# Two products issued later in the gating heads, and six landing places instead of three for the output weights of layer A

## The chip, the cores and the metric

The kernel runs on one core of a Trainium2 chip. The metric is the device time of one execution, in microseconds. Before the change it is 2045.86 us, the median of three runs (2043.93 to 2048.65). The core has an engine for matrix products (TensorE, PE in the profile; its weight loads are PEld), a vector engine (VectorE, DVE), a scalar engine (ScalarE, ACT), a general engine (GpSimd, POOL) and a queue that here only starts DMAs (SyncE, SP). Each engine runs its own instructions strictly in program order and waits for the others by semaphores.

## The reference, cut to what matters

Two layers, each `x <- x + norm(mixer(norm(x)))`, on x of 1024 x 1024 floats. Layer A is a gated unit, layer B dilated attention. Only layer A and its end matter here:

```
z = h @ w_in;  u, v, g = split(z)            # 2048 columns each
v = layer_norm(gelu(v), vn_g, vn_b)          # over 2048 columns
sg = w_s[h] @ v[chunk, head h] + b_s[h]      # 16 heads, 8 chunks of 128 rows
y = gelu(u) * sg * silu(g);  out = y @ w_out # 2048 -> 1024
x = x + rms_norm(out) * ...;  h for layer B = rms_norm(x)
```

## The kernel before, in words

**Precision.** Each fp32 operand is split into a high part and the rest, and each product is three matmuls (high x high, high x rest, rest x high). The splits cost ACT one copy and DVE one subtraction for each 128 x 512 tile.

**The order.** It is written by a small planner (class `Plan`): every matmul that is emitted moves a clock of its own forward, and actions put into a heap with `plan.at` or `plan.after` are emitted, on whatever engine they belong to, when that clock passes their time. These times only set the order of instructions; the engines run as fast as their waits let them.

**Pieces.** Weights (and, at the end of layer A, the rows of y) come as pieces of 128 x 512 through class `Pieces`. A piece from DRAM is loaded by SP into a landing place, a tile `raw` of which there are three; ACT and DVE split it into a tile `wt` (eight of them, so splitting runs up to eight pieces ahead of TensorE); when the split is emitted its place counts as free and the next load is emitted. The load waits on its queue until the split has really happened. `source(raw, nr, lo_pool, slack)` tells the object where places come from, how many there are, which pieces GpSimd splits, and how long a place is kept back after its split.

**Heads of layer A (`head`, line 792; `spatial`, line 673).** For each of 16 heads, u and g come from seven products in Strassen's manner (forms a11, a12, s2, s1, s3, a22, s4; 12 matmuls of 512 columns each), of which partial sums x in a PSUM bank psD are copied out by ACT (`snap`) before the next form adds to them. Beside the next head's products the planner puts the spatial part of the head: `ws_tr` transposes w_s[h] (tile wsr), ACT and DVE split it into `wst`; `ws_sum` multiplies it by a matrix of ones, to get row sums, and DVE makes t (from psT, the factors vgb and the bias bsr); `v_load`, `v_norm`, `v_split` bring v (tiles vr, vs); `mix` multiplies vs by wst (psS), and DVE makes sg and the product ya, which `y_out` stores. `ws_load`, on ACT's queue, fetches w_s and b_s of the head after the next. `vgb_tr` (line 631) transposes the norm factors vn_g and vn_b once, before the first use of vgb. The form tiles of the heads, and the pieces of summed weights, lie in a pool `fm`.

**End of layer A (line 932 on).** Four blocks (two halves of the rows, two halves of the columns), each of 16 steps; a step takes a piece of y and a piece of w_out and issues 12 matmuls into four banks. At the end of a block ACT copies each bank out (yo) and squares it. The banks of the blocks are DDOO, SSTT, DDOO, DDSS. After blocks two and four, `post` emits for each of four row tiles the norm, the residual, the second norm and the transposes of h for layer B (psT from xr), on DVE, ACT and TensorE. Then layer B's values are computed (`v_bank`) from 16 pieces of four loads each, in banks psD again.

Of the kernel before, what the change touches and what calls it, by code (L numbers as in the profile page):

```python
# [12 lines left out]
F32 = mybir.dt.float32  # L13
# [8 lines left out]
P = 128  # L22
# [196 lines left out]
def encoder_block(ctx: ExitStack, tc: tile.TileContext, x, norm_pre, norm_post, a_w_in, a_w_s,  # L219
# [8 lines left out]
    plan = Plan()  # L228
# [12 lines left out]
    pc = Pieces(nc, plan, lambda: wpool.tile([P, 2, 512], F32R, name="wt"), 8)  # L241

    def bank(tag):
        return ps.tile([P, 512], F32, name="ps" + tag, tag=tag)
# [7 lines left out]
    def bcast_row(ap, off, n):  # L252
        return bass.AP(tensor=ap.tensor, offset=ap.offset + off, ap=[[0, P], [1, n]])
# [23 lines left out]
    def bmm(o, l, r, start, stop):  # L277
        mm(o, l, r, start, stop)

    def tr(o, i):  # L280
        nc.tensor.transpose(o, i, ident)  # L281
        plan.now += 0.109

    def act(o, i, f=AF.Copy, **k):
        nc.scalar.activation(o, i, f, **k)  # L285

    def tt(o, a, b, op, e=None):
        (e or nc.vector).tensor_tensor(o, a, b, op=op)  # L288

    def stt(o, a, s, b, op0, op1):  # L290
        nc.vector.scalar_tensor_tensor(o, a, s, b, op0=op0, op1=op1)  # L291
# [66 lines left out]
    def new_h():  # L358
        return (hpool.tile([P, 8, S], F32R, name="hTh", tag="hTh"),
                hpool.tile([P, 8, S], F32R, name="hTl", tag="hTl"))  # L360
# [114 lines left out]
    for i in range(8):  # L475
        b = bank("D")
        for k in range(8):
# [5 lines left out]
            while n > 0 and norms:  # L483
                weight, f = norms.pop(0)
# [36 lines left out]
    fms = ExitStack()  # L521
# [111 lines left out]
        nc.tensor.transpose(b[:, :2 * NH], vrow, ident[:2 * NH, :2 * NH])  # L633
        act(vgb.rearrange("p a h -> p (a h)"), b[:, :2 * NH])

    plan.after(2.0, vgb_tr)

    def dense_cols(o, w, s0, n):

# [31 lines left out]
    def spatial(h, ug, t0):  # L671
        vs, T = {}, ws.pop(h)

        def ws_tr():
            b = bank("T")
            tr(b[:, :128], T["w"])
            T["wt"] = sp.tile([P, 2, P], F32R, name="wst")
            act(T["wt"][:, 0], b[:, :128])
            tt(T["wt"][:, 1], b[:, :128], T["wt"][:, 0].bitcast(F32), OP.subtract)

        def ws_sum():
            b = bank("T")
            bmm(b[:, :256], ones, T["wt"].rearrange("p a q -> p (a q)"), True, True)
            T["t2"] = sp.tile([P, P], F32, name="t2")
            stt(T["t2"], b[:, :128], vgb[:, 1, h:h + 1], T["b"], OP.mult, OP.add)
            stt(T["t2"], b[:, 128:256], vgb[:, 1, h:h + 1], T["t2"], OP.mult, OP.add)

        def v_load():
            vs["r"] = sp.tile([P, 8, P], F32, name="vr", bufs=1)
            nc.sync.dma_start(vs["r"], va[h])  # L690

        def v_norm(i):
            act(vs["r"][:, i], vs["r"][:, i], AF.Identity, scale=lnr[:, i:i + 1], bias=lnb[:, i:i + 1])

        def v_split(e):
            if e == 0:
                vs["v"] = sp.tile([P, 2, 8, P], F32R, name="vs", bufs=1)
                act(vs["v"][:, 0], vs["r"])
            else:
                tt(vs["v"][:, 1], vs["r"], vs["v"][:, 0].bitcast(F32), OP.subtract)  # L700

        def mix(cc):
            b = bank("S")
            for k in range(2):
                c = 2 * cc + k
                bmm(b[:, 256 * k:256 * k + 256], vs["v"][:, 0, c], T["wt"].rearrange("p a q -> p (a q)"),
                    True, False)
                bmm(b[:, 256 * k:256 * k + 256], vs["v"][:, 1, c], T["wt"].rearrange("p a q -> p (a q)"),
                    False, True)
            g = sp.tile([P, 2, P], F32, name="sg")  # L710
            b4 = b.rearrange("p (c a q) -> p c a q", c=2, a=2)
            t2 = T["t2"][:, None, :].to_broadcast([P, 2, P])
            stt(g, b4[:, :, 0], vgb[:, 0, h:h + 1], t2, OP.mult, OP.add)
            stt(g, b4[:, :, 1], vgb[:, 0, h:h + 1], g, OP.mult, OP.add)

            if cc == 0:
                vs["y"] = sp.tile([P, S], F32, name="ya", bufs=1)
            y = vs["y"].rearrange("p (t c b) -> p c t b", t=8, c=8)[:, 2 * cc:2 * cc + 2]
            tt(y, g.rearrange("p c (b t) -> p c t b", t=8),
               ug[:, 256 * cc:256 * cc + 256].rearrange("p (c b t) -> p c t b", c=2, t=8), OP.mult)  # L720
            if cc == 3:
                plan.after(2.0, y_out)

        def y_out():
            nc.sync.dma_start(ya[h], vs["y"])
            done_a.add(h)
            pc.pump()

        plan.at(t0, v_load)
        plan.at(t0 + 0.2, ws_tr)  # L730
        for i in range(8):
            plan.at(t0 + 3.5 + 0.35 * i, v_norm, i)
        plan.at(t0 + 6.5, v_split, 0)
        plan.at(t0 + 7.6, v_split, 1)
        plan.at(t0 + 2.5, ws_sum)
        plan.at(t0 + 4.0, ws_load, h + 2)
        return mix

    def y_a(kt, sh):
# [23 lines left out]
    lo_pool = set()  # L763
# [42 lines left out]
    def head(h, mixes):  # L806
        if h + 1 < NH:
            plan.after(0.8, w_load, h + 1)
        u = sp.tile([P, S], F32, name="us")
        c0, c1 = slice(0, 512), slice(512, 1024)  # L810
        x, z, y = bank("D"), bank("O"), None
        g = {}

        def snap(nm):
            g[nm] = sp.tile([P, 512], F32, name=nm, bufs=1)
            act(g[nm], x)

        def gate(c, o, nm):

            g[c] = g[nm]  # L820
            tt(g[c], o, g[nm], OP.add)

        def gated(c, i):
            tt(u[:, c], u[:, c], g[i], OP.mult)

        form_mm(x, "a11", True)
        snap("p1")
        form_mm(z, "a12", True)
        tt(u[:, c0], z, g["p1"], OP.add)
        form_mm(x, "s2")  # L830
        snap("u2")
        y = bank("O")
        form_mm(y, "s1", True)
        form_mm(x, "s3")
        snap("u3")
        gate(1, y, "u3")
        for f in mixes[:2]:
            f()
        form_mm(x, "a22")
        act(u[:, c1], x, AF.Gelu_apprx_tanh)  # L840
        act(u[:, c0], u[:, c0], AF.Gelu_apprx_tanh)
        for f in mixes[2:3]:
            f()
        form_mm(y, "s4")
        gate(0, y, "u2")
        for f in mixes[3:]:
            f()
        for dt, c in ((0.0, 1), (0.9, 0)):
            plan.after(dt, act, g[c], g[c], AF.Silu)
        plan.after(1.4, gated, c1, 1)  # L850
        plan.after(2.4, gated, c0, 0)
        mix = spatial(h, u, plan.now + 0.5)
        return [lambda cc=cc: mix(cc) for cc in range(4)]

    mixes = []
    for h in range(NH):
        mixes = head(h, mixes)
    plan.after(10.0, lambda: [f() for f in mixes])


    def out_mm(b, y, w, t, first, last):
# [57 lines left out]
    def open_chain():  # L919
        plan.until(lambda: len(done_a) == NH)  # L920
        sps.close()
        fms.close()
        cp["pool"] = chs.enter_context(tc.tile_pool(name="cp", bufs=2, side="right", reuse_waits="tile"))
        cp["gp"] = cp["pool"].tile([P, D], F32, name="gp", bufs=1)
        nc.sync.dma_start(cp["gp"], bcast_row(norm_post, 0, D))
        cp["gq"] = cp["pool"].tile([P, D], F32, name="gq", bufs=1)
        nc.sync.dma_start(cp["gq"], bcast_row(norm_pre, D, D))
        cp["n"] = 0
        hnew["h"], hnew["l"] = new_h()
        pc.source(raw, 3)  # L930

    plan.after(25.0, open_chain)
    for sh, ch, tags in ((0, 0, "DDOO"), (0, 1, "SSTT"), (1, 0, "DDOO"), (1, 1, "DDSS")):
        bs = [bank(t) for t in tags]
# [13 lines left out]
                post(4 * sh + t, POST_EVERY[sh][0] + POST_EVERY[sh][1] * t)  # L948


    pc.source(raw, 3, lo_pool, 2.0)
    hTh, hTl = hnew["h"], hnew["l"]

    def v_alloc():
# [479 lines left out]
    def open_b2():  # L1434
        chs.close()
        st = ExitStack()
        B2["s"] = st
        B2["p"] = st.enter_context(tc.tile_pool(name="b2", bufs=2, side="right", reuse_waits="tile"))


    for t in range(0, 8, 2):
        for c in range(4):
            vch.setdefault(c, [])
            v_bank(c, t, t == 6, None if c else lambda i: plan.until(lambda: cp["n"] > i))
    plan.drain()
    open_b2()
    xws.close()
    b1s = ExitStack()
    b1 = b1s.enter_context(tc.tile_pool(name="b1", bufs=2, reuse_waits="tile"))

# [175 lines left out]
```

## Time and profile before

| what | value |
|---|---|
| median of three runs | 2045.86 us |
| the profiled execution, its span | 2045.38 us, 2043.6 us |
| TensorE, its weight loads | 96%, 81% of the span |
| DVE, ACT, GpSimd | 65%, 54%, 16% |
| heads of layer A | about 203 to 578 us |
| end of layer A, four blocks | 578.1 to 797 us |

TensorE is busy nearly throughout; what it loses is in short waits, and in stretches in which its granted clock is at the lower of its two levels, 1.2 GHz instead of 2.4 GHz (a granted clock of 0.83 over 20 us means that it was at the half for 6.8 us of them, so that 3.4 us are lost beside the waits).

### The profile page before, as it was taken

Reading aid. Unit: us, or ns where it says so; the run is one execution under the profiler, and the core shown is the slowest. Engines: PE = TensorE matmul, PEld = TensorE weight load, DVE = VectorE, ACT = ScalarE, POOL = GpSimd, SP = SyncE. Lnnn points to the kernel's source line nnn. Section 1 sums busy time; section 2 is a strip of 40 time slices with the busy share of each in tenths; the row PEclk is TensorE's granted clock in tenths of the full one; section 3 lists DMA queues with packets and bytes.
Section 4 is the critical chain, followed back from the end, with each engine's and each line's share of the span. In section 5 each row is a group of like instructions: output and inputs, shape, how many; then the busy total and the mean of one; then the engine's idle time right before and its main releaser. Section 6 shows DMA issues by size and latency. Waiting matters only on the chain.

```text
span 2043.6 us, 30630 instructions
## 1 busy us (share of the span) xinstructions
PE 1962.9 (96%) x10617; PEld 1665.1 (81%) x10617; DVE 1325.6 (65%) x3051; ACT 1108.5 (54%) x2455; POOL 332.9 (16%) x394
## 2 busy tenths in 40 slices
PE   8999899999989988999999999999999999999998
PEld 5887777777767667999898888898888888787876
DVE  6455577787764576526567576585675766868747
ACT  5223466666654455225656665656566556576722
POOL 0001322232100000011003021130120310413121
PEclk9999999999989999999999999999999999999999
DMA  4334444433245556331223142241331422313277
GB/s 174 105 114 125 126 142 127 133 122 99 87 134 181 185 191 203 107 115 50 76 77 106 52 112 66 70 129 47 101 102 52 114 64 86 113 47 104 79 222 273
DMA packets 246024, 235.57 MB, mean 115 GB/s; under 512 B 18843, under 2 KB 203835, under 8 KB 245868
## 3 DMA queue, kind: packets, MB, share of 16 engines
q1 hardware_dynamic: 235068, 219.97, 35.4%
q10 hardware_dynamic: 10800, 13.63, 1.9%
q8 instruction: 84, 1.38, 0.3%
q14 instruction: 72, 0.59, 0.1%
HBM read 188.03 MB, written 57.04 MB: 120 GB/s over the span
## 4 chain that ended last, share of the span: by engine, by line
PE 68%; DVE 14%; DMA 9%; ACT 4%; issue 3%; SPq 0%; POOL 0%; ACTq 0%; DVEq 0%
PE psD L270 50%; PE psO L270 8%; PE psS L270 5%; DVE wt L178 4%; PE psT L281 3%; DMA raw<-in_a_w_out_dram 3%; DVE sg L291 3%; PE psT L270 2%; ACT wt L176 1%; DMA raw<-ya 1%; DVE ya L288 1%; DMA toep<-vec 1%; DVE o L288 1%; DMA raw<-in_b_w_in_dram 1%; DMA vr<-va 1%
## 5 line engine op out<-in xcount | busy, mean ns | idle before, releaser
L270 PE MATMUL psD<-hTh,wt 128*128 128x512 f32 x2176 | 722.3, 396 | 3.7 <-ACT u L285 3.6
L270 PEld LDWEIGHTS psD<-hTh,wt 128*128 128x128 f32 x2176 | 401.1, 189 | 72.2 <-ACT u L285 4.5
L270 PE MATMUL psD<-hTl,wt 128*128 128x512 f32 x1088 | 433.3, 398 | 0.0
L270 PE MATMUL psD<-wt,hTh 128*128 128x256 f32 (+1 forms) x1760 | 360.6, 301 | 9.6 <-ACT psD L285 4.9
L178 DVE TENSOR_TENSOR wt<-raw,wt 128x512 fp32r<-128x512 f32 x316 | 215.2, 702 | 190.2 <-ACT wt L176 188.3
L270 PEld LDWEIGHTS psD<-wt,hTh 128*128 128x128 f32 x1760 | 285.2, 193 | 21.7 <-ACT psD L285 5.3
L176 ACT ACTIVATE wt<-raw 128x512 fp32r<-128x512 f32 x328 | 197.7, 627 | 189.0 <-DMA raw<-in_a_w_out_dram 53.0
L285 ACT ACTIVATE xs<-xs,st 128x256 f32<-128x256 f32 (+2 forms) x384 | 176.7, 461 | 174.9 <-DVE st L1155 173.8
L270 PE MATMUL psD<-wt,hTl 128*128 128x256 f32 (+1 forms) x880 | 265.7, 302 | 0.8 <-DVE hTl L288 0.8
L270 PEld LDWEIGHTS psD<-hTl,wt 128*128 128x128 f32 x1088 | 205.3, 189 | 33.4
L270 PEld LDWEIGHTS psD<-wt,hTl 128*128 128x128 f32 x880 | 169.3, 192 | 6.7 <-DVE hTl L288 2.1
L288 DVE TENSOR_TENSOR pt<-psT,pt 128x512 fp32r<-128x512 f32 (+1 forms) x192 | 115.0, 599 | 85.2 <-ACT pt L285 82.4
L1155 DVE CUSTOM_DVE_ANT_0 xs<-psS,bias 128x256 f32<-128x256 f32 (+1 forms) x256 | 95.8, 411 | 60.3 <-PE psS L270 58.2
L1081 POOL TENSOR_SCALAR ks<-ks 64x512 fp32r<-64x512 f32 x96 | 59.6, 621 | 432.2 <-ACT ks L285 428.4
L270 PEld LDWEIGHTS psO<-pt,vs 128*128 128x128 f32 (+1 forms) x640 | 99.1, 177 | 24.7 <-DVE pt L288 8.4
L288 DVE TENSOR_TENSOR ks<-psD,ks 64x512 fp32r<-64x512 f32 x96 | 66.1, 689 | 79.4 <-ACT ks L285 77.8
L270 PE MATMUL psO<-pt,vs 128*128 128x256 f32 (+1 forms) x640 | 108.1, 282 | 5.6 <-DVE pt L288 4.4
L270 PE MATMUL psS<-ks,qs 128*128 128x256 f32 x640 | 109.3, 285 | 0.0
L285 ACT ACTIVATE pt<-psT 128x512 fp32r<-128x512 f32 (+1 forms) x192 | 100.0, 521 | 14.5 <-PE psT L281 11.6
L281 PE MATMUL psT<-ident,xs 128*128 128x128 f32 x640 | 103.2, 273 | 3.4 <-ACT xs L285 2.6
L270 PEld LDWEIGHTS psS<-ks,qs 128*128 128x128 f32 x640 | 97.5, 188 | 10.2 <-DVE ks L288 0.2
L285 ACT ACTIVATE ks<-psD 64x512 fp32r<-64x512 f32 x96 | 57.1, 594 | 80.6 <-PE psD L270 79.1
(218 smaller groups left out, 3196.7 us busy)
## 6 DMA issues: line engine op xcount, KB each, us to landing
raw<-in_b_w_in_dram SPq DMA_DIRECT2D x160, 256.0 KB, 3.0
wb<-in_a_w_in_dram SPq DMA_DIRECT2D x64, 256.0 KB, 5.2
raw<-ya SPq DMA_DIRECT2D x64, 256.0 KB, 3.0
raw<-in_a_w_out_dram SPq DMA_DIRECT2D x64, 256.0 KB, 3.1
y<-yd SPq DMA_DIRECT2D x56, 256.0 KB, 5.5
cb<-sc SPq DMA_DIRECT2D x64, 192.0 KB, 4.9
raw<-in_a_w_in_dram SPq DMA_DIRECT2D x32, 256.0 KB, 4.4
va<-vst SPq DMA_DIRECT2D x32, 256.0 KB, 3.8
```

The costliest lines, as they stand in the source:

```text
L176: self.nc.scalar.activation(hi, src, AF.Copy)
L178: e.tensor_tensor(lo, src, hi.bitcast(F32), op=OP.subtract)
L270: nc.tensor.matmul(o, l, r, start=start, stop=stop, skip_group_check=more)
L281: nc.tensor.transpose(o, i, ident)
L285: nc.scalar.activation(o, i, f, **k)
L288: (e or nc.vector).tensor_tensor(o, a, b, op=op)
L291: nc.vector.scalar_tensor_tensor(o, a, s, b, op0=op0, op1=op1)
L1081: nc.gpsimd.tensor_scalar(place(u, u.k[a][:, 0], o, o + 64, hh), hi.bitcast(F32), 1.0, 0.0, op0=OP.mult, op1=OP.add)
L1155: nc.vector.tensor_tensor_reduce(out=o, in0=s_, in1=bi, op0=OP.add, op1=OP.min, scale=1.0, scalar=3.0e38, accum_out=col(0, t))
```

## The change

Three order times move: `ws_sum` from 2.5 to 6.2 and `ws_load` from 4.0 to 7.6 after the start of the spatial part, `vgb_tr` from 2.0 to 12.0, and the mixing products that follow the last head from 10.0 to 14.0. The pool `fm` is closed right after the heads, and a pool of six places `raw6` is opened there; the pieces use it from that point until the last round of the first values of layer B, where the three places and the slack of 2.0 come back (before, the slack began with the end of the four blocks).

```diff
-    plan.after(2.0, vgb_tr)
+    plan.after(12.0, vgb_tr)
...
-        plan.at(t0 + 2.5, ws_sum)
-        plan.at(t0 + 4.0, ws_load, h + 2)
+        plan.at(t0 + 6.2, ws_sum)
+        plan.at(t0 + 7.6, ws_load, h + 2)
...
-    plan.after(10.0, lambda: [f() for f in mixes])
+    plan.after(14.0, lambda: [f() for f in mixes])
+    fms.close()
+    rps = ExitStack()
+    rp = rps.enter_context(tc.tile_pool(name="rp", bufs=6, reuse_waits="tile"))
+    pc.source(lambda: rp.tile([P, 512], F32, name="raw6"), 6)
...
         sps.close()
-        fms.close()
...
         hnew["h"], hnew["l"] = new_h()
-        pc.source(raw, 3)
...
-    pc.source(raw, 3, lo_pool, 2.0)
+    pc.lo_pool = lo_pool
...
     for t in range(0, 8, 2):
+        if t == 6:
+            pc.source(raw, 3, lo_pool, 2.0)
...
     xws.close()
+    rps.close()
```

On TensorE, at the first spatial part (head 0's, beside head 1's products): psT<-wst,ones is the product of `ws_sum`, psO the form a12, psD the form s2. Before:

```order
L270 MATMUL psO<-hTh,wt 128x512
L270 MATMUL psO<-hTl,wt 128x512
L270 MATMUL psT<-wst,ones 128x256
L270 MATMUL psO<-hTh,wt 128x512 x2
L270 MATMUL psO<-hTl,wt 128x512
```

The same place after the change:

```order
L270 MATMUL psO<-hTl,wt 128x512
L270 MATMUL psO<-hTh,wt 128x512 x2
L270 MATMUL psO<-hTl,wt 128x512
L270 MATMUL psO<-hTh,wt 128x512
L270 MATMUL psD<-s_701,wt 128x512 x7
L270 MATMUL psT<-wst,ones 128x256
L270 MATMUL psD<-s_701,wt 128x512 x5
```

The product of ones stands behind 19 matmuls of the two forms instead of 2, so 17 later.

On ACT, in head 0: vgb is the copy of the transposed norm factors, p, u are the copies of psD after the forms a11, s2 and (the second u) s3, wt<-wb and wt<-tw are splits of the next head's weights and of sums of them. Before:

```order
L669 DMA bsr<-in_a_b_s_dram 128x128
L285 ACTIVATE vgb<-psT 128x32
L285 ACTIVATE p_1659<-psD 128x512
L285 ACTIVATE u_1691<-psD 128x512
L176 ACTIVATE wt<-wb 128x512 x2
L176 ACTIVATE wt<-tw 128x512 x2
L176 ACTIVATE wt<-wb 128x512
L285 ACTIVATE u_1735<-psD 128x512
```

After:

```order
L669 DMA bsr<-in_a_b_s_dram 128x128
L285 ACTIVATE p_1656<-psD 128x512
L285 ACTIVATE u_1688<-psD 128x512
L176 ACTIVATE wt<-wb 128x512 x2
L176 ACTIVATE wt<-tw 128x512 x2
L176 ACTIVATE wt<-wb 128x512
L285 ACTIVATE vgb<-psT 128x32
L285 ACTIVATE u_1735<-psD 128x512
```

The copy vgb moves behind the five splits, and ahead of the copy u of form s3.

On SP, where the last head's v is fetched (vr<-va) among the pieces for the end of layer A. Before:

```order
L160 DMA raw<-ya 128x512
L690 DMA vr<-va 128x1024
L725 DMA ya<-ya 128x1024
L160 DMA raw<-in_a_w_out_dram 128x512
L160 DMA raw<-ya 128x512
```

After (the numbered raw tiles are places of the new pool):

```order
L160 DMA raw_4850<-ya 128x512
L160 DMA raw_4852<-in_a_w_out_dram 128x512
L160 DMA raw_4854<-ya 128x512
L160 DMA raw_4859<-in_a_w_out_dram 128x512
L690 DMA vr<-va 128x1024
L725 DMA ya<-ya 128x1024
```

Three more loads of pieces stand ahead of vr.

## Rows read from the trace of the kernel before

**Rows 1.** The page's first part: busy time, share of the span, instructions.

```profile
PE 1962.9 (96%) x10617; PEld 1665.1 (81%) x10617; DVE 1325.6 (65%) x3051; ACT 1108.5 (54%) x2455; POOL 332.9 (16%) x394
```

**Rows 2.** Waits of TensorE, 250 to 600 us: total, times, longest, us.

```profile
PE psT L270 <- DVE wst L288: 15.1, 12, 1.8
PE psD L270 <- ACT u L285: 2.9, 1, 2.9
PE psS L270 <- ACT vs L285: 2.8, 1, 2.8
PE psS L270 <- DVE sg L291: 1.1, 2, 0.7
PE psS L270 <- DVE vs L288: 0.9, 1, 0.9
```

**Rows 3.** Timeline of TensorE around 486 us: start, length, [idle before <- releaser].

```profile
486.50 0.39 PE L270 MATMUL psT<-wst,ones 128*128 128x256 f32 x1 [1.81 <-DVE wst L288]
```

**Rows 4.** Timeline of DVE, the same head.

```profile
486.16 0.28 DVE L288 TENSOR_TENSOR wst<-psT,wst 128x128 fp32r<-128x128 f32 x1
```

**Rows 5.** Timeline of ACT, the same head.

```profile
485.25 0.58 ACT L285 ACTIVATE p<-psD 128x512 f32<-128x512 f32 x1
```

**Rows 6.** Windows: length, busy PE PEld DVE ACT POOL, PEclk, DMA share, GB/s.

```profile
200.00:220.00 20.00, 14.97 (x52) 11.38 (x51) 9.68 (x32) 6.51 (x14) 5.06 (x4) 0.83 0.69 193
480.00:500.00 20.00, 18.19 (x79) 14.59 (x79) 13.34 (x22) 11.02 (x22) 3.95 (x4) 0.91 0.37 112
560.00:580.00 20.00, 17.11 (x76) 13.82 (x75) 11.39 (x20) 13.44 (x24) 0.00 (x0) 0.91 0.25 83
580.00:600.00 20.00, 15.26 (x62) 12.09 (x62) 13.64 (x26) 8.67 (x18) 0.00 (x0) 0.83 0.45 150
597.85:797.00 199.15, 179.33 (x756) 139.03 (x755) 114.80 (x236) 96.31 (x183) 0.00 (x0) 0.97 0.58 184
724.00:744.00 20.00, 13.81 (x56) 9.78 (x55) 16.03 (x41) 11.95 (x27) 0.00 (x0) 0.90 0.64 214
820.00:830.00 10.00, 8.85 (x62) 8.86 (x63) 6.65 (x24) 3.07 (x7) 0.00 (x0) 0.83 0.47 158
```

**Rows 7.** Waits of TensorE, 600 to 820 us.

```profile
PE psD L270 <- ACT psD L285: 9.1, 3, 4.9
PE psT L281 <- issue: 3.3, 2, 1.8
PE psT L281 <- DVE xr L291: 1.7, 1, 1.7
```

**Rows 8.** Waits of ACT, 600 to 800 us.

```profile
ACT wt L176 <- DMA raw<-in_a_w_out_dram: 52.3, 39, 3.9
ACT wt L176 <- DMA raw<-ya: 29.5, 23, 3.0
```

**Rows 9.** DMA issues: KB each, median us to landing.

```profile
raw<-ya SPq DMA_DIRECT2D x64, 256.0 KB, 3.0
```

**Rows 10.** Timeline of TensorE at the end of layer A, six matmuls a row.

```profile
602.17 1.52 PE L270 MATMUL psD<-wt 128*128 128x512 f32 x6
603.53 1.52 PE L270 MATMUL psO<-wt 128*128 128x512 f32 x6
```

**Rows 11.** Timeline of TensorE in head 0.

```profile
208.47 0.28 PE L633 MATMUL psT<-ident,vrow 32*128 32x32 f32 x1 [5.03 <-DMA vrow<-in_a_vnorm_b_dram]
...
223.95 0.50 PE L270 MATMUL psD<-hTh,wt 128*128 128x512 f32 x1 [0.74 <-ACT u L285]
```

**Rows 12.** Timeline of GpSimd in head 0, third of four sums.

```profile
215.77 1.29 POOL L288 TENSOR_TENSOR wb<-wb 128x512 f32<-128x512 f32 x1
```

**Rows 13.** Timeline of ACT in head 0.

```profile
208.79 0.20 ACT L285 ACTIVATE vgb<-psT 128x32 f32<-128x32 f32 x1 [4.98 <-PE psT L633]
...
220.54 0.63 ACT L176 ACTIVATE wt<-wb 128x512 fp32r<-128x512 f32 x1 [0.17 <-issue]
223.30 0.60 ACT L285 ACTIVATE u<-psD 128x512 f32<-128x512 f32 x1 [2.13 <-PE psD L270]
```

## The prediction

> **What bounds the kernel now.** I read the page's busy times first: TensorE is busy 96% of the span [rows 1], so only what delays TensorE counts. Then TensorE's waits by stretch, because an average over the span hides them. In the heads there is one repeated wait, the product of ones on DVE's subtraction wst: 15.1 us in 12 waits [rows 2]. The timeline shows how it looks from inside [rows 3 to 5]: TensorE comes to the product at 484.7, DVE, in order behind other work, does wst only at 486.16. Third, the windows with the granted clock: after several waits the clock falls to its lower level, 1.2 of 2.4 GHz, for some us, and a clock of 0.91 over 20 us loses another 1.8 us, 0.83 loses 3.4 [rows 6]. Last, who keeps TensorE waiting at the end of layer A: it waits for ACT to empty psD (9.1 us), for transposes' inputs (5.0 us) [rows 7], and ACT in turn sits 81.8 us in 62 waits for pieces to land [rows 8]. That is the mark of too few places, since a piece takes 3.0 us to land [rows 9].
>
> **How much the four blocks can give.** From 597.85 to 797, 722 of the 768 matmuls run (46 stand ahead of the last head's mixing products in program order). Six take 1.36 us where nothing waits [rows 10], so 722 x 1.36 / 6 = 163.7 us, plus 32 transposes at 0.1 us, my estimate (a quarter of the columns, and about as much again for the start), 3.3 us: 167.0. The stretch lasts 199.1 us [rows 6], so 32.1 us are lost there. TensorE's idle time says 199.15 - 179.33 = 19.8 us only, since a slow matmul and a restart count as busy [rows 6].
>
> The Trainium skill (Perfetto Trace Analysis, Identifying the Most-Contended Engine) warns of just this: matmul busy time is a poor measure of the headroom, and weight-load time is a better one. Here weight loads are busy 139.0 us of the 199.15 [rows 6], which agrees that more is free than 19.8. By idle time alone the fourth term below would be 12 us smaller and the sum 2007.
>
> **The change part by part.**
>
> *Product of ones later (heads).* It moves 17 matmuls back, 17 x 0.227 = 3.9 us by the pitch of [rows 10]. The longest wait is 1.81 us [rows 3], so all 12 are covered with 2 us to spare: -15.1. The slow clock at 480 to 500 follows the 1.81 us wait; with it goes -1.8 [rows 6]. Behind the product nothing is urgent: its user, the mixing products, comes a form and more later. What is late next is the copy p, which must be out before form s2: it ends at 485.83 [rows 5], s2 could start at about 486.9 (ten matmuls after 484.7), so 1 us is left. `ws_load` moves past the v_norm copies on ACT, and its b_s DMA waits for DVE's t as before, but the copy of form s2 is then ahead of it: nothing. The 2.9 us wait on ACT's u [rows 2] hangs on vr of a head whose place on SP doesn't move; it stays. Term: -16.9, bounds -10 (that 1 us gone, and p late by half a microsecond in every head) and -16.9.
>
> *Norm factors later (head 0).* Gone is TensorE's wait of 5.03 us for vrow [rows 11] and the slow clock behind it, 3.4 us [rows 6] (200 to 220). But fixed work is now late. On ACT the copy of form s3 stands behind five splits of head 1's weights, and the fifth needs GpSimd's third sum, which ends at 215.77 + 1.29 = 217.06 and hangs on a DMA that starts no earlier than before [rows 12]. Then 0.63 + 0.20 + 0.60 us on ACT [rows 13] put the release of the next form at 218.6, while TensorE would be there at about 215.0 (50 matmuls after 203.4, where the wait began). So it waits 3.6 us; the form starts at 218.6 instead of 223.95 [rows 11], -5.3. A wait of 2.9 us cost 1.8 us of clock at 560 to 580 [rows 2, 6]; I charge that again. Term: -3.5, bounds 0 and -8.4.
>
> *Mixing products of the last head later.* They cost 2.8 + 0.9 + 1.1 = 4.8 us of waits [rows 2] and 3.4 us of clock [rows 6] (580 to 600). 18 more matmuls stand ahead of them, 4.1 us, about as long as vs was late (3.7). But its source vr now queues on SP behind three more loads of 256 KB, 3.7 us at 214 GB/s (724 to 744 [rows 6]), partly made up since these loads wait for no place. I take vr 2 us late and the 1.1 us on DVE's sg as before, and one slow stretch of 1.8: 8.2 - 4.9. Term: -3.3, bounds 0 and -7.1.
>
> *Six places.* Each place is bound by 3.0 us of landing and 0.63 of ACT's copy at the least [rows 9, 13]; three give a piece each 1.2 us before issue and subtraction are added, against 1.36 us that TensorE needs; six halve that. ACT's 81.8 us of waiting should go, and with it the late copies of psD at the ends of blocks three and four, where the next products use psD at once. What is then late is DVE: at 724 to 744 it is busy 16.0 of 20 us while TensorE does only 13.8 us of work [rows 6], so at full speed DVE is over its limit there for a while. Splits run eight pieces ahead, 8 x 1.36 = 10.9 us, which covers it; the transposes' inputs have no such cover. Of the 32.1 us I keep 2.5 for transposes, 3 at the two block ends, 3 of small waits and 1.8 of clock: 10.3. Term: -21.8, bounds -8 and -32.
>
> *Behind the blocks.* At 820 to 830 TensorE waits for splits and loses 1.7 us of clock, 2.9 us in all (10 - 8.85 idle, and 0.17 x 10) [rows 6]; those pieces are now split in one run of ten on ACT. That run, ahead of the first copy of a bank of values, takes 10 x 0.63 = 6.3 us [rows 13], against some 10 us (96 matmuls of half the columns) until the bank is needed again. The slow clock behind the last block end goes on past 797 for about 2 us. Term: -5 together, bounds 0 and -6. No row shows a run of ten, hence the 0.
>
> The sum: -16.9 - 3.5 - 3.3 - 21.8 - 5.0 = -50.5. The profiled execution took 2045.4, so 1994.9; the median of the runs is 0.5 above that: 1995.
>
> **Rivals.**
>
> 1. *DVE takes over.* It is busy 13.3 of 20 us in the heads [rows 6] and in order, so a wait that goes at the product of ones may return at p or at the mixing products, and the transposes stay late. For it: the overload at 724 to 744. Against: a third of DVE's time in the heads is free. Half the heads' term and 10 of the blocks, 3 behind: -8.5 - 3.5 - 3.3 - 10 - 3 = -28.3, 2018.
> 2. *The DMAs are the bound, and the change to six does nothing.* For it: the stretch already moves 184 GB/s [rows 6], and the pieces alone need 256 KB in 1.36 us, 193 GB/s, with x and the stored x1 on top. Against: the DMA engines are busy 0.58 of the time, and 0.64 at 214 GB/s. Only the first three terms stay: -23.7, 2022.
> 3. *Slower.* Six loads in flight slow each other, beside the row loads and stores of `post`, so that throughput in the blocks drops. 120 pieces are 31.5 MB; it decides once the stretch lasts 223 us, that is below 141 GB/s, where it eats the first three terms. At 120 GB/s the stretch takes 262 us, +63 - 24: 2085. For it: nothing but that six were never seen here; against it the 214 GB/s with share 0.64.
> 4. *All cover holds.* Each term at its lower bound: -16.9 - 8.4 - 7.1 - 32 - 6 = -70.4, 1975.
>
> **Chances.** Forecast 0.65 (own range 1983 to 2008), DVE 0.17, DMA bound 0.09, all cover 0.06, slower 0.03. The range that leaves out the slower case, the last half of rival 4 and little more is 1980 to 2022. What a measurement of this kernel can tell from no change is 0.2%, 4.1 us, so all but rival 3 are faster: faster 0.95, same 0.02 (several terms given back at once, none of the cases above), slower 0.03.
>
> **What would show each step.** No wait on wst in the heads, and heads 22 us apart instead of 23.4 (375 us for 16); a wait of TensorE on ACT's copy u of 3 to 4 us near 215; the wait on vs under 2 us; ACT's waits on raw below 20 us between the heads and layer B, psD waits below 3; the four blocks some 190 us or less instead of 219. I am wrong if ACT still waits for pieces with six places, if the heads keep their pitch, or if DVE's lateness shows up as waits of the transposes and of the weights' use.

## The result and the profile after

The changed kernel takes 1988.42 us (median of four runs, 1985.48 to 1990.80), the kernel before 2046.07 in the same runs: ratio 0.9717, interval 0.9698 to 0.9737. The forecast was 1995, and the measured time lies in the range of the forecast alone (1983 to 2008). The profiled executions differ by 58.8 us (2045.38 and 1986.57).

The order of stages is the same and both traces hold 10617 matmuls, so I compared the start of the n-th matmul in both. The lead over the kernel before, at places named by their time there:

| place in the trace of before, us | lead, us | what the stage since the last row gave | I had said |
|---|---|---|---|
| 190.0, ahead of the heads | -1.0 | 1.0 lost; no part of the change lies there | 0 |
| 240.1, behind head 0 | 4.3 | 5.3 | 3.5 |
| 578.1, end of the heads | 23.4 | 19.0 | 16.9 |
| 620.1, behind the last head's mixing products | 24.4 | 1.0 | 3.3 |
| 797.4, end of the four blocks | 54.0 | 29.6 | 21.8 |
| 830.3, behind the first values | 59.2 | 5.2 | 5.0 |
| 2034.8, the last matmul | 58.8 | -0.3 | 0 |

Busy times on the page of the changed kernel, against [rows 1]: TensorE does the same work and is busy for 20 us less, so a third of what was saved had stood there as work.

```profile
PE 1942.6 (98%) x10617; PEld 1660.8 (84%) x10617; DVE 1326.7 (67%) x3051; ACT 1101.0 (55%) x2455; POOL 337.3 (17%) x394
```

TensorE's waits in the changed kernel, 190 to 560 us (us in total, times, longest):

```profile
PE psD L270 <- ACT u L285: 5.5, 3, 2.6
PE psD L270 <- ACT p L285: 1.2, 1, 1.2
PE psO L270 <- DVE u L288: 0.3, 1, 0.3
```

and 560 to 780 us, which goes to the end of the four blocks and past it:

```profile
PE psS L270 <- DVE sg L291: 3.9, 2, 3.5
PE psT L281 <- issue: 0.7, 1, 0.7
PE psS L270 <- DVE vs L288: 0.7, 1, 0.7
PE psD L270 <- ACT vst L285: 0.5, 1, 0.5
```

The twelve waits on wst [rows 2] are gone, and so are the 9.1 us on psD and the 1.7 on xr [rows 7]. New are 3.5 us on sg and a wait of 2.56 us on u, at another head than before.

One head answers to [rows 3 to 5]. DVE's timeline (start, length, instruction), TensorE's and ACT's:

```profile
472.22 0.28 DVE L288 TENSOR_TENSOR wst<-psT,wst 128x128 fp32r<-128x128 f32 x1
```

```profile
473.88 0.28 PE L270 MATMUL psT<-wst,ones 128*128 128x256 f32 x1
474.00 1.33 PE L270 MATMUL psD<-s,wt 128*128 128x512 f32 x5
```

```profile
471.26 0.58 ACT L285 ACTIVATE p<-psD 128x512 f32<-128x512 f32 x1
```

The product of ones comes 1.4 us after wst is there (473.88 less 472.50), without a wait.

Windows, with the columns of [rows 6] (length, busy PE, PEld, DVE, ACT, POOL, granted clock, DMA share, GB/s). Before, the heads behind head 0 and the blocks:

```profile
240.08:578.10 338.02, 319.99 (x1485) 260.61 (x1484) 257.30 (x409) 216.02 (x376) 81.35 (x52) 0.99 0.37 115
620.08:797.37 177.29, 157.47 (x663) 121.11 (x662) 103.37 (x218) 88.57 (x171) 0.00 (x0) 0.97 0.58 183
```

The same matmuls in the changed kernel, and two stretches of 20 us:

```profile
235.75:554.75 319.00, 314.75 (x1485) 260.76 (x1484) 261.01 (x409) 214.76 (x377) 83.56 (x52) 0.99 0.39 123
595.72:743.39 147.67, 146.96 (x664) 121.19 (x662) 99.55 (x217) 83.05 (x169) 0.00 (x0) 1.00 0.68 218
200.00:220.00 20.00, 17.46 (x73) 13.05 (x73) 14.47 (x35) 9.36 (x18) 6.77 (x5) 1.00 0.76 220
670.00:690.00 20.00, 20.00 (x95) 16.51 (x94) 18.67 (x46) 10.39 (x20) 0.00 (x0) 1.00 0.77 248
```

In the blocks TensorE now loses 0.7 us of 147.67 and keeps its full clock. ACT's waits there, 570 to 744 us, against the 81.8 us of [rows 8]: it waits for TensorE, and 1.3 us for a piece.

```profile
ACT wt L176 <- PE psO L270: 33.0, 18, 8.4
...
ACT wt L176 <- DMA raw<-ya: 1.3, 1, 1.3
```

### The profile page after: what moved, and what is told of

Read it like the earlier page. It is cut to its first block, busy times and chain, and to the rows that moved or that the text cites. A ratio compares the mean times of both kernels' runs of the same rounds, so it can differ in the third digit from the quotient of the medians.

```text
span 1984.8 us, 30678 instructions
## 1 busy us (share of the span) xinstructions
PE 1942.6 (98%) x10617; PEld 1660.8 (84%) x10617; DVE 1326.7 (67%) x3051; ACT 1101.0 (55%) x2455; POOL 337.3 (17%) x394
## 4 chain that ended last, share of the span: by engine, by line
PE 85%; DVE 6%; DMA 3%; ACT 3%; issue 1%; POOL 1%; SPq 0%; ACTq 0%; DVEq 0%; POOLq 0%
PE psD L270 57%; PE psO L270 13%; PE psS L270 8%; PE psT L281 4%; PE psT L270 3%; DVE wt L178 1%; DVE o L288 1%; DMA vr<-va 1%; DMA va<-vst 0%; ACT wt L176 0%; DVE sg L291 0%; DMA raw<-in_b_w_in_dram 0%; DMA ya<-ya 0%; DVE xs L1157 0%; POOL o L288 0%
## 5 line engine op out<-in xcount | busy, mean ns | idle before, releaser
L178 DVE TENSOR_TENSOR wt<-raw,wt 128x512 fp32r<-128x512 f32 x316 | 210.1, 699 | 155.7 <-ACT wt L176 154.4
L270 PEld LDWEIGHTS psD<-wt,hTh 128*128 128x128 f32 x1760 | 281.9, 191 | 15.5 <-DVE wt L178 3.6
L176 ACT ACTIVATE wt<-raw 128x512 fp32r<-128x512 f32 x328 | 191.3, 624 | 144.3 <-PE psD L270 50.0
```

Of the source, the lines that this page charges most:

```text
L176: self.nc.scalar.activation(hi, src, AF.Copy)
L178: e.tensor_tensor(lo, src, hi.bitcast(F32), op=OP.subtract)
L270: nc.tensor.matmul(o, l, r, start=start, stop=stop, skip_group_check=more)
```

## Two places where the changed kernel still waits

**Head 5.** ACT's timeline; ACTq is the queue on which it issues DMAs. The first row is the load of wsr one head earlier, toep a load for layer B:

```profile
298.69 0.33 ACTq L667 DMA_DIRECT2D wsr<-in_a_w_s_dram  x1
...
314.81 0.61 ACTq L511 DMA_DIRECT2D toep<-vec  x1
...
320.23 4.67 ACTq L667 DMA_DIRECT2D wsr<-in_a_w_s_dram  x1
324.99 1.00 ACTq L669 DMA_DIRECT2D bsr<-in_a_b_s_dram  x1
326.04 1.15 ACT L176 ACTIVATE wt<-wb 128x512 fp32r<-128x512 f32 x2 [5.22 <-issue]
...
328.65 0.57 ACT L285 ACTIVATE u<-psD 128x512 f32<-128x512 f32 x1
```

TensorE, at the form that needs u:

```profile
329.28 0.50 PE L270 MATMUL psD<-hTh,wt 128*128 128x512 f32 x1 [2.56 <-ACT u L285]
```

An issue that takes 0.33 us elsewhere takes 4.67 here, and five splits and the copy u stand behind it. SP issues its four loads of w at that moment and is slow there too, against 2.16 us for four one head earlier:

```profile
300.00 2.16 SPq L572 DMA_DIRECT2D wb<-in_a_w_in_dram  x4
...
321.15 0.34 SPq L690 DMA_DIRECT2D vr<-va  x1
321.54 7.35 SPq L572 DMA_DIRECT2D wb<-in_a_w_in_dram  x4
```

At its old order time the load of wsr was issued before toep, vr and these loads; the change put it behind toep, which is 1536 KB here, and beside SP's loads.

**The last head.** SP issues vr at 557.20, behind six loads of pieces; it lands at 563.9. ACT sits in front of it:

```profile
563.88 2.42 ACT L285 ACTIVATE vr<-vr,lnb,rs 128x128 f32<-128x128 f32 x6 [4.66 <-DMA vr<-va]
...
569.12 3.21 ACT L176 ACTIVATE wt<-raw 128x512 fp32r<-128x512 f32 x6
```

DVE, in order, has to do the six subtractions that ACT's wait held back before it comes to sg:

```profile
570.39 3.69 DVE L178 TENSOR_TENSOR wt<-raw,wt 128x512 fp32r<-128x512 f32 x6
574.00 0.48 DVE L291 SCALAR_TENSOR_TENSOR sg<-psS,vgb,t 128x256 f32<-128x256 f32 x1
```

## The experiments

### Each part alone, on the kernel before

**Heads alone.**

```diff
-        plan.at(t0 + 2.5, ws_sum)
-        plan.at(t0 + 4.0, ws_load, h + 2)
+        plan.at(t0 + 6.2, ws_sum)
+        plan.at(t0 + 7.6, ws_load, h + 2)
```

> Only the product of ones and the load of the mixing weights are moved (2.5 to 6.2, 4.0 to 7.6). Theory A, the terms add up: the 15 heads behind the first shrink as in the changed kernel, by about 19 us, the twelve waits on wst are gone, and the rest keeps its length: 2027 us (2023 to 2030). In one head the issue of the load of mixing weights on ACT's queue takes several us (4.67 in the changed kernel, 0.33 elsewhere), and TensorE waits some 2.6 us on the copy u behind it. Theory B, the terms lean on each other: the heads give only what my bound said, about 10 us, since the shorter heads meet the late source of a later head: 2036 us.

Measured: 2028.06 us, ratio 0.9914 (0.9896 to 0.9931), 18.4 us between the places 240.1 and 578.1. No wait on wst, and the slow issue in the same head (4.68 us, wait on u 2.57). Theory A.

**Norm factors alone.**

```diff
-    plan.after(2.0, vgb_tr)
+    plan.after(12.0, vgb_tr)
```

> Only the transpose of the norm factors is moved (2.0 to 12.0). Theory A, it acts alone: the wait of 5.0 us for vrow goes, and a wait on ACT's copy u of 1 to 4 us comes near 215; matmuls from 240 us on stand 5 us earlier than before and stay so: 2041 us (2038 to 2043). Theory B, the slow clock stays behind the new wait: 1 to 2 us, 2044 us.

Measured: 2043.60 us, ratio 0.9994 (0.9982 to 1.0006). Neither theory as I wrote it: the lead is 5.1 us at the place 240.1, then 2.8 at 358.6, 1.2 at 472.1 and 0.6 at 541.4. TensorE's waits in this kernel, 240 to 580 us:

```profile
PE psT L270 <- DVE wst L288: 18.5, 11, 2.5
```

They were 15.1 [rows 2]; the two other kernels that keep the old heads have 15.5 (mixing products alone) and 14.3 (six places alone). One wait of 1.9 us, at 251.5, has a slow stretch of 3.4 us behind it that the kernel before does not have there. So the heads with the early product of ones take back what head 0 gives them; the run below that undoes this edit alone tests it.

**Mixing products of the last head alone.**

```diff
-    plan.after(10.0, lambda: [f() for f in mixes])
+    plan.after(14.0, lambda: [f() for f in mixes])
```

> Only the mixing products of the last head are moved (10 to 14). In the changed kernel this place gave 1 us where I had said 3.3. Theory A, the six places took the rest: with six places six splits stand in a row on DVE ahead of sg, and TensorE waits 3.5 us for it. With three places there is no such row: alone it gives 3 to 5 us, 2042 us. Theory B, the late source vr is the cause, with three places as with six: it gives 1 us or less, 2045 us, and sg is late here too.

Measured: 2046.99 us, ratio 1.0006 (0.9993 to 1.0019). Theory A falls: with three places sg is late all the same. TensorE in this kernel:

```profile
599.62 1.19 PE L270 MATMUL psS<-wst,vs 128*128 128x256 f32 x4 [5.18 <-DVE sg L291]
```

ACT there, held up by vr first:

```profile
586.36 2.42 ACT L285 ACTIVATE vr<-vr,lnb,rs 128x128 f32<-128x128 f32 x6 [3.63 <-DMA vr<-va]
```

and DVE, with the last subtraction in front of sg, waiting for ACT, which waited for a piece:

```profile
597.87 0.69 DVE L178 TENSOR_TENSOR wt<-raw,wt 128x512 fp32r<-128x512 f32 x1 [0.54 <-ACT wt L176]
598.48 0.48 DVE L291 SCALAR_TENSOR_TENSOR sg<-psS,vgb,t 128x256 f32<-128x256 f32 x1
```

Theory B has the size, but only part of the cause: the late vr holds ACT's splits back by 3.6 us, yet vs is ready here by 592.8, and the last splits ahead of sg come one by one, paced by three places. Further back in the order the products have more splits ahead of them on DVE, and wait for whatever those wait for: pieces and vr here, vr in the changed kernel.

**Six places alone** (the new pool and the changed calls of `source`). The order times are as before; they are four, where the section on the change announces three.

> Only the six places, with the mixing products at 10 as before. Theory A: the four output blocks and the stretch behind them give what they gave in the changed kernel, 29.6 and 5.2 us, and nothing before them changes: 2011 us (2008 to 2015); ACT waits less than 5 us for pieces to land in the blocks. Theory B, the DMAs or DVE bind once the heads before are as slow as they were: 20 us or less, 2025 us or more.

Measured: 2012.32 us, ratio 0.9834 (0.9816 to 0.9851); 29.7 us between 620.1 and 797.4 and 5.7 behind; ACT waits 0.4 us for a piece there. Theory A: neither the DMAs nor DVE bind.

By the ratios the four alone give 17.6, 1.2, -1.2 and 33.9 us, together 51.5; all together give 57.9. Of the 6.4 us between them some 4 are the norm factors (1.2 alone, 4.8 when undone, below); the rest lies within the intervals, which are 2.5 to 3.6 us a side.

### The changed kernel with one thing undone or resized

**Norm factors back at 2.0.**

```diff
-    plan.after(12.0, vgb_tr)
+    plan.after(2.0, vgb_tr)
```

> The changed kernel with the transpose of the norm factors back at 2.0. Alone this edit gave 5.1 us by 240 us and had given it back by 541 us (2043.6 against 2044.1). Theory A, it was given back to the waits on wst, which hold the pitch of the old heads; where they are gone the 5 us stay. Then this kernel is 5 us slower than the changed one: 1993.5 us (1991 to 1996), and the lag stands in one step near 208 us and doesn't shrink. Theory B, the edit is worth nothing in either kernel: 1988.5 us, the lag shrinks to nothing before 541.

Measured: 1993.19 us, ratio 0.9743 (0.9715 to 0.9772), 4.8 us more than the changed kernel's median. The lead is 1.0 at the place 240.1 where the changed kernel has 4.3, 19.7 at 578.1 (23.4) and 54.7 at 830.3 (59.2). Theory A: the gain stays once nothing in the heads takes it back.

**Mixing products back at 10.**

```diff
-    plan.after(14.0, lambda: [f() for f in mixes])
+    plan.after(10.0, lambda: [f() for f in mixes])
```

> The changed kernel with the mixing products of the last head back at 10. Alone this edit was worth nothing (2047.0 against 2044.1), with sg 5.2 us late. Theory A, it is vr, late on SP, that holds up ACT and DVE, and the place of the products only chooses which wait shows it: within 2 us of the changed kernel, 1988 to 1991 us; the waits stand on vs (3 us or more) in place of sg. Theory B, with six places the later place is worth the 3.3 us that I forecast: 1992 us.

Measured: 1988.65 us, ratio 0.9717 (0.9688 to 0.9745): no difference. The wait is 3.6 us on ACT's vs now, in place of 3.5 on sg. Theory A.

**Four places.**

```diff
-    rp = rps.enter_context(tc.tile_pool(name="rp", bufs=6, reuse_waits="tile"))
-    pc.source(lambda: rp.tile([P, 512], F32, name="raw6"), 6)
+    rp = rps.enter_context(tc.tile_pool(name="rp", bufs=4, reuse_waits="tile"))
+    pc.source(lambda: rp.tile([P, 512], F32, name="raw6"), 4)
```

> The changed kernel with four places in place of six, ahead of the same point. Theory A, a place is held for landing (3 to 4 us), the copy (0.63) and the subtraction (0.65), some 5.2 us, so four places give a piece each 1.3 us, just under the 1.36 that TensorE needs: within 4 us of the changed kernel, 1988 to 1992 us, ACT's waits for pieces 10 to 40 us. Theory B, pieces come in runs and the planner pairs them, so that more room than the mean is needed: four places lose a third or more of the 35 us: 2000 us or more, and psD waits at the block ends come back.

Measured: 1992.60 us, ratio 0.9736 (0.9703 to 0.9770), just outside what A said and far from B. ACT's waits in this kernel, 570 to 750 us:

```profile
ACT wt L176 <- DMA raw<-ya: 33.2, 23, 4.2
...
ACT wt L176 <- DMA raw<-in_a_w_out_dram: 7.6, 11, 1.5
```

Half of ACT's waiting is back and nearly all of it is covered: between 620.1 and 750.0 this kernel gains 19.3 us, the changed one 23.2. The 3.9 between them are a wait of 2.1 us on psD and a slow stretch of 3.4 behind it.

**The load of the mixing weights at its old time, with three places for bsr** (the old time with two would wait for the later product's user).

```diff
-            T["b"] = sp.tile([P, P], F32, name="bsr")
+            T["b"] = sp.tile([P, P], F32, name="bsr", bufs=3)
...
-        plan.at(t0 + 7.6, ws_load, h + 2)
+        plan.at(t0 + 4.0, ws_load, h + 2)
```

> The changed kernel with the load of the mixing weights back at 4.0, which three places for bsr in place of two make possible, so that its two DMAs on ACT's queue are issued ahead of SP's four loads of w and not beside them. Theory A, the 4.67 us that ACT spent on one issue came from standing beside SP's loads: no issue on ACT's queue over 1.5 us behind 215, no wait of 2.6 us on u and no slow clock near 330: 4.3 us less, 1984 us (1982 to 1987). Theory B, the issue is held up at this head wherever it stands, or another wait takes its place: 1988 us.

Measured: 1981.76 us, ratio 0.9687 (0.9659 to 0.9715). The same head, ACT's queue and then SP's:

```profile
314.36 0.34 ACTq L667 DMA_DIRECT2D wsr<-in_a_w_s_dram  x1
314.74 0.44 ACTq L669 DMA_DIRECT2D bsr<-in_a_b_s_dram  x1
```

```profile
321.20 7.75 SPq L572 DMA_DIRECT2D wb<-in_a_w_in_dram  x4
```

SP is as slow as before, where TensorE does not wait for it; ACT is out of its way, and the wait of 2.56 us and the slow stretch are gone. All that theory A forecast comes, at a time just below its range. The cause that it names is not shown: in this order the load of wsr also stands ahead of toep again, which is issued at 315.34. By the matmul count 4.3 us come from it in the heads (23.3 us between 240.1 and 578.1 against 19.0); the medians say 6.7, and 5.0 against the repeated run below.

### What the two places cost

**vr of the last head earlier.** The load is emitted ahead of the form a22 of the last head and not behind its last form:

```diff
+        vs = {}
+        if h == NH - 1:
+            v_load(h, vs)
         form_mm(x, "a22")
...
-        plan.at(t0, v_load)
+        if h < NH - 1:
+            plan.at(t0, v_load, h, vs)
```

> The changed kernel with the last head's source vr asked for one form and a half earlier, ahead of six loads of pieces on SP in place of behind them. Theory A, vr is what makes the last head's end late: it lands near 552 in place of 563.8, ACT doesn't wait 4.7 us for it, DVE's six subtractions are done before sg is due, the waits on vs (0.7) and sg (3.9) and the slow stretch near 573 (6.8 us at half clock, 3.4) go: 7 to 8 us less, 1980.5 us (1979 to 1984). Theory B, the six subtractions stand ahead of sg on DVE in program order all the same and make it late: 3 us less at most, 1986 us or more.

Measured: 1981.36 us, ratio 0.9702 (0.9681 to 0.9722). SP in this kernel, and TensorE:

```profile
546.04 0.38 SPq L673 DMA_DIRECT2D vr<-va  x1
```

```profile
571.11 0.71 PE L270 MATMUL psS<-wst,vs 128*128 128x256 f32 x4 [1.19 <-DVE sg L291]
```

ACT does not wait for vr, and the slow stretch near 573 is gone. Two waits on sg stay, 2.1 us in all. By the matmul count 4.7 us come from it (5.7 us between 578.1 and 620.1 against 1.0); the medians say 7.1, and 5.4 against the repeated run below. Theory A, with sg not quite gone and less than its 7 to 8 us in the stage itself.

**Both.** The last two edits together.

> The changed kernel with the earlier vr of the last head and the load of the mixing weights at 4.0 with three places for bsr. Theory A, the two are apart in time and add up: 6.7 us (as measured for the load alone) and 7 to 8: 1974 us (1972 to 1978). Theory B, the heads' end is bound by DVE as soon as one is gone, and only the larger stays: 1981 us.

Measured: 1979.37 us, ratio 0.9685 (0.9669 to 0.9702). The median is lower than either alone by some 2 us only, between my two theories. By the matmul count the two give 7.3 us more than the changed kernel (23.2 against 19.0 in the heads, 4.1 against 1.0 in the next stage), where alone they gave 4.3 and 4.7; the median says 7.4 against the repeated run below. The difference is a slow stretch: between 560 and 580 the granted clock is 0.91 here and 1.00 in the kernel with the earlier vr alone, behind the same two waits on sg.

**And the second load of weights behind head 0's first copies.**

```diff
     ws_load(0)
-    ws_load(1)
+    plan.after(9.0, ws_load, 1)
```

> As the last, and the second of the two loads of mixing weights at the heads' start is issued 9 us later, behind the copies p and u and four splits on ACT. Theory A, in head 0 the issue of bsr (at 207.5 in the changed kernel) stands ahead of p on ACT and makes it late: the wait of 1.2 us on p goes and the one on u stays: 1973 us, 1 us less than the last. Theory B, the issue now delays the split that the next form or u needs: the waits of head 0 grow by 1 us or more, 1975 us.

Measured: 1976.87 us (1976.65 to 1977.23), ratio 0.9674 (0.9658 to 0.9689): the fastest of all, 11.5 us below the changed kernel's first median, 9.9 below that of its run beside this one and 2.5 below the last kernel. Theory A's mechanism holds: the wait on p is gone, the one on u stays (1.4 us), and head 0 gives 6.7 us where it gave 5.3. Its 1973 us started from a time for the last kernel that was not reached. TensorE's waits, 190 to 780 us:

```profile
PE psD L270 <- ACT u L285: 2.9, 2, 1.5
PE psS L270 <- DVE sg L291: 2.1, 2, 1.2
PE psT L281 <- issue: 0.7, 1, 0.7
PE psO L270 <- DVE u L288: 0.3, 1, 0.3
```

**The changed kernel again.**

> The changed kernel itself beside the three variants, on the same chip: 1988 us (1985 to 1991), with the same four places in its trace: one issue of 4 to 5 us on ACT's queue near 320, the wait on u of 2.6 us behind it, sg 3.5 us late at the last head, and two or three slow stretches between 200 and 800.

Measured: 1986.73 us, ratio 0.9724 (0.9704 to 0.9744). The slow issue is there again (4.87 us at 320.71, wait on u 2.8), sg is 3.5 us late, and there is one more slow stretch, near 546, behind a wait of 2.0 on u. The heads give 16.9 us in this trace, and 18.4 to 19.0 in the six others with the product and the load where the change puts them: one trace tells that stage to some 2 us only. The four blocks are steadier, 29.6 to 29.7 us in every trace with six places.

## Why the prediction was right, step by step

**Product of ones: right, too small by what a wait costs beside its idle time.** -16.9 said, -19.0 measured (18.4 alone). The windows of the heads show three parts. Idle time falls from 18.0 us to 4.3, so 13.8: the 15.1 I counted, less 1.4 by which the waits on u grew. The clock gives 1.7: two slow stretches of 3.4 before, one after. The remaining 3.5 are busy time of TensorE (319.99 to 314.75, less those 1.7), some 0.3 us for each of the twelve waits. The matmul ahead of the wait of [rows 3], and the one behind the product:

```profile
484.31 0.39 PE L270 MATMUL psO<-hTl,wt 128*128 128x512 f32 x1
...
486.72 0.63 PE L270 MATMUL psO<-hTh,wt 128*128 128x512 f32 x2
```

The one ahead counts as busy for its whole 0.39 us, where in flow the next starts 0.23 us after it: 0.16. The product takes 0.39 us behind a wait and 0.28 in flow, and the matmul behind it starts 0.22 us after it and not 0.12 (474.00 less 473.88): 0.10. Behind that the pitch is 0.23 as in flow, until the clock falls here. Twelve times 0.26 is 3.1 of the 3.5. I had charged a wait at its idle time alone. The margin of the copy p held.

**`ws_load` at nothing: wrong.** I asked what b_s waits for, and not what the queues carry at the new time: toep ahead on ACT's own, four loads beside it on SP's. The move cost 2.56 us of wait and a slow stretch, 4.3 us by the count; it hides inside the -19.0, and gross the heads gave 23.3 (load_early, 240.1 to 578.1).

**Norm factors: right in place and release, wrong on the clock.** I had put the release of the next form at 218.6; the copy u ended at 219.09 and the form began at 219.15. TensorE waits 1.29 us there and not 3.6, since it had waited 1.24 for p and came later; p stood behind the second issue of bsr on ACT, and the kernel that moves that issue has no such wait. The 1.8 us of clock that I charged did not come (1.00 in the window 200 to 220), and without them my 5.3 is the measured 5.3. That they agree so well is in part luck: counted from the heads' start the form came 5.8 us earlier, and 0.5 were lost again behind it. What I did not see is that this term holds only together with the first: alone it was given back. I added terms up that are not independent.

**Mixing products: wrong.** -3.3 said, nothing measured either way (1.0006 alone, 1988.65 against 1988.42 when undone). I let 18 more matmuls cover the late vs and kept sg's waits at 1.1 us. But the order time moves the products on DVE too, behind more splits, and those splits had been held back on ACT by the same late vr. The wait changed its name and kept its size. Where vr is issued 11 us earlier, 4.7 us go.

**Six places: the mechanism right, the size too careful.** -21.8 said, -29.6 measured, near my bound of -32. (Over my own stretch, 597.85 to 797, the lead grows by 25.3 us, because the later mixing products and their waits now fall into it.) I kept 10.3 us for transposes, block ends, small waits and a slow stretch; 0.7 us of wait was left, and no slow stretch. Of the 5.0 us that I read as waits for transposes' inputs, 3.3 are put down to "issue" [rows 7], where the profile shows no releaser; the 0.7 are what is left of those. I read DVE's 16.0 of 20 us [rows 6] as a sign that it would be over its limit. At 670 to 690 it does 18.67 of 20 us while TensorE does 20.00 without a wait: the eight split pieces ahead were cover enough. The Trainium skill (Perfetto Trace Analysis, Identifying the Most-Contended Engine) calls matmul busy time a poor measure of what is free; here the idle time of the blocks, 19.8 us [rows 6], was less than the 29.6 that could be had, while the weight loads, 121 us before and after, rose from 0.68 of the stretch to 0.82.

**Behind the blocks: right** (-5.2 for -5). Between 797.37 and 830.33 the granted clock was 0.88 and TensorE idle for 2.1 us; over the same matmuls it is 1.00 and 0.5 now. Whether the places or the later slack gave it, no run separates.

The rivals: DVE does not take over (the waits on sg at the last head, 3.9 us, are all that points that way), the DMAs moved 218 GB/s in the blocks and were not the bound, nothing was slower. The result lies between the forecast and the rival in which all cover holds.

## What to carry to other kernels

A gain ahead of the heads was kept only once the heads no longer set their pace by waits; so try such edits together before adding them up. When an instruction is moved later because TensorE waits for its source, see what stands ahead of its users on every other engine: if the source itself is late, the wait only changes its name, and asking for the source earlier is the edit. A DMA issued on a computing engine's queue is an instruction in that engine's order, so put it where nothing urgent stands behind it, and look at what that queue is still carrying.

## What the hardware did that I had not expected

The issue of a 64 KB load (128 x 128 fp32) on ACT's queue took 4.67 us at one head and 0.33 to 0.4 us at most others, in every trace that has it at the later order time (4.67 to 4.87 us, six kernels). The Trainium skill (Perfetto Trace Analysis, DMA Instruction — HWDGE (DVE, Sync)) says that the shown length holds a wait for a descriptor generator which two queues share and lock. The trace agrees only in part: SP's issue of vr took its usual 0.34 us at 321.15, in the middle of ACT's.

What sets this head apart is the size of toep, which ACT's queue had issued 5.4 us earlier. The sizes of its issues at 314.81 and 383.82 in the changed kernel:

```profile
toep<-vec ACTq DMA_DIRECT2D x1, 1536.0 KB
...
toep<-vec ACTq DMA_DIRECT2D x1, 768.0 KB
```

Behind the second, at head 8, wsr was issued in 0.37 us (0.33 to 1.09 in the other traces), and behind one of 512 KB in 0.33. SP's four loads of w show the same in all fourteen traces: they take 7.35 to 8.16 us where they come 5 to 7 us behind 1536 KB of toep, 5.01 to 5.59 behind 768 KB, and 2.0 to 3.9 where toep is 14 us or more away. It is so in the kernel before, where wsr is issued ahead of toep and takes 0.33 us; toep goes out there at 290.16 (768 KB), 327.70 (1536) and 395.93 (768):

```profile
309.44 2.08 SPq L572 DMA_DIRECT2D wb<-in_a_w_in_dram  x4
332.77 7.67 SPq L572 DMA_DIRECT2D wb<-in_a_w_in_dram  x4
...
401.01 5.05 SPq L572 DMA_DIRECT2D wb<-in_a_w_in_dram  x4
```

So the slow issues go with a large load issued shortly before, and standing beside SP's loads, which wsr does at other heads too, is not enough. No run moves toep, so this is not shown to be the cause, and how it would hold up an issue stays open.

Whether a wait is followed by a slow stretch differs between traces. A wait of 2.56 us on u at 329.28 was followed by one (3.4 us), and the same waits in five other traces, 2.57 to 2.77 us, came with one too; in the kernel with the mixing products at 10 the wait of 2.63 us did not. TensorE's row of that kernel and its window, at a granted clock of 1.00:

```profile
327.01 0.50 PE L270 MATMUL psD<-hTh,wt 128*128 128x512 f32 x1 [2.63 <-ACT u L285]
```

```profile
320.00:340.00 20.00, 17.37 (x84) 14.32 (x83) 15.28 (x25) 12.66 (x24) 3.47 (x3) 1.00 0.50 172
```

So the clock is a cost to be given a chance, not a sum to be added to each wait.
